# Time mixing with the inverse applied to the removal keys before the chain, and keys and removal keys stacked

## The chip, the cores and the metric

The kernel runs on one core of a Trainium2 chip. Its engines work side by side, each through its own queue in order: TensorE (PE, with its weight loads as PEld), VectorE (DVE), ScalarE (ACT), GpSimd (POOL), and SyncE (SP), which issues the transfers. The metric is the device time of one execution in microseconds (us). Lower is better.

## The reference

Two layers of a streaming encoder, over 64 frames of a running stream, 16 learned tokens and 1024 frames of a new stream. In each layer one projection feeds three groups of heads: a short gated convolution, latent attention, and RWKV-7 time mixing with four heads of 64. Their outputs go through one output projection. The change is in the time mixing, which is, per head and token:

```python
def step(s, inp):
    r_t, w_t, k_t, v_t, kk_t, a_t = inp
    sa = jnp.einsum('bhvk,bhk->bhv', s, -kk_t)
    s = (s * w_t[:, :, None, :] + sa[..., None] * (kk_t * a_t)[:, :, None, :]
         + v_t[..., None] * k_t[:, :, None, :])
    return s, jnp.einsum('bhvk,bhk->bhv', s, r_t)
```

The state `s` is decayed by `w`, loses what it holds along the removal key `kk`, gains `v` along `k`, and is read by `r`. A group norm over each head, a bonus term and a gate follow.

## The kernel before

Tokens are taken in chunks of 64. A pass (`rwkv_prep`, `rwkv_scan`, `rwkv_finish`) takes 384 tokens, which is six chunks, of two heads on 128 partitions. A layer has six passes: three token groups for each of two head pairs. Two layers make twelve passes and 72 chunks. Four of the chunks hold the learned tokens, which start from an empty state.

`rwkv_prep` forms, for the whole pass, the decays, the scaled removal keys `ar` (with the scaled `r` beside them), the keys `kt` and the write-back keys `bb`, and turns `v`, `bb` and `kt` so that tokens lie on partitions (`tm`, three transposes each). The products within a chunk are `x` (masked into `X1` for `bb` and `X2` for `kt`) and `av` (`X2` with the values). The triangular matrix in `X1` is inverted into `Q`: blocks of 16 on VectorE with a way through memory (`tri`), then block steps on TensorE (`inv`).

`rwkv_scan` then walks the six chunks in order. A chunk is a chain of three steps, each a visit to TensorE and one to VectorE. `xp` multiplies the removal keys with the state and adds `av`. `up` multiplies the inverse `Q` with that. `sp` multiplies the turned keys with `v` and the turned write-back keys with the result of `up`; VectorE adds the decayed state. At the end of the pass `yp` forms the output from the states (`ss`), `X2` with `v`, and `X1` with the results of `up`. These three share one PSUM bank (`rs`, one buffer); `rwkv_prep` uses two (`rw`).

The order is written by a planner while the program is built. `Meter` keeps a reckoned time for each engine. Time mixing is a set of side streams; each `yield` names the data and the bank that the next step needs. After each matmul of the main work, `pump` inserts the side steps whose needs are reckoned to be ready (`due`). The main work is the input projection of the layer (`prj`, 24 weight tiles of 128 columns and one smaller, in three token groups), and after it attention with the first half of the output projection (`race`). `self.solo` becomes true when the side streams are done, and gives attention more banks. `evict` copies out of PSUM on whichever of ScalarE and VectorE is reckoned to be free first.

Of the kernel before, what the change touches and what calls it, by code (L numbers as in the profile page):

```python
# [31 lines left out]
GN = 384  # L32
# [4 lines left out]
BLK = 16  # L37
# [154 lines left out]
class Net:  # L192
# [689 lines left out]
    def rwkv(self, l):  # L882

        parts = [(g, hp) for hp in range(2) for g in range(3)]
        self.state = [None, None]
# [24 lines left out]

    def rwkv_tag(self, i):
        return "z"

    def rwkv_prep(self, l, i, g, hp):
        nc, I, O = self.nc, self.I, self.O
# [15 lines left out]
        wa, wb = S("wa"), S("wb")  # L931
        e1, e2, a = (wa[:, GN * x:GN * (x + 1)] for x in range(3))
        ar = wb[:, 0:2 * GN].rearrange("p (i t) -> p i t", i=2)
        kk, rn, bb = wb[:, 0:GN], wb[:, GN:2 * GN], wb[:, 2 * GN:3 * GN]
        ch = lambda x: x.rearrange("p (c t) -> p c t", t=64)
        wt = S("wt")
        tm = [wt[:, GN * i:GN * (i + 1)] for i in range(3)]

        def turned(d, src):
# [20 lines left out]
        yield bb, "rw"  # L960
        turned(tm[0], v)
# [10 lines left out]
        for t in range(3):  # L972
# [5 lines left out]
        nc.gpsimd.tensor_copy(dc, ch(e1)[:, :, 63])  # L978
        yield a, kk, e2
        nc.vector.tensor_tensor(out=bb, in0=kk, in1=a, op=ALU.mult)  # L980
        nc.vector.tensor_tensor(out=bb, in0=bb, in1=e2, op=ALU.mult)
        nc.vector.scalar_tensor_tensor(out=ch(kk)[:, :, 1:64], in0=ch(kk)[:, :, 1:64], scalar=-1.0, in1=ch(e1)[:, :, 0:63],
                                       op0=ALU.mult, op1=ALU.mult)
        nc.vector.tensor_scalar(ch(kk)[:, :, 0:1], ch(kk)[:, :, 0:1], -1.0, None, op0=ALU.mult)
        nc.gpsimd.tensor_tensor(out=rn, in0=r, in1=e1, op=ALU.mult)
# [33 lines left out]
        chunks(X1, bb, C_X1)  # L1019
# [9 lines left out]
        chunks(X2, kt, C_X2)  # L1029
# [22 lines left out]
        spread = lambda x: x.unsqueeze(2).to_broadcast([128, 6, 4, BLK])  # L1052
# [6 lines left out]
        for y, d, o in ((1, dq, Q), (2, dt, Tm)):  # L1059
            nc.vector.tensor_tensor(out=o.rearrange("p t (b k) -> p t b k", k=BLK), in0=spread(d), in1=blk, op=ALU.mult)  # L1060
# [34 lines left out]
        yield (Q,)  # L1095
        self.made = dc, wb, wt, wq, wx

    def rwkv_scan(self, l, i, g, hp, dc, wb, wt, wq, wx):

        nc, I, O = self.nc, self.I, self.O  # L1100
        state = self.state
        rp = lambda s: self.ps(s, "rs")
        ar = wb[:, 0:2 * GN].rearrange("p (i t) -> p i t", i=2)
        vT, bT, kT = (wt[:, GN * i:GN * (i + 1)].rearrange("p (t f) -> p t f", t=3) for i in range(3))
        v4 = lambda x, n: x.rearrange("p (j t n) -> p j t n", j=2, n=n)
        X1, X2 = v4(wq[:, 0:768], 128), v4(wx[:, 0:768], 128)
        Q = X1[:, :, :, 0:64]
        AV, UU = v4(wq[:, 768:1152], 64), wx[:, 768:1152].rearrange("p (t f) -> p t f", t=3)
        quad = [(t, c) for t in range(3) for c in range(2)]
        cs = lambda t, c: slice(128 * t + 64 * c, 128 * t + 64 * c + 64)  # L1110
        cr = lambda c: slice(64 * c, 64 * c + 64)
        ss = self.S(self.rwkv_tag(i), "ss")[:, 0:768].rearrange("p (c n) -> p c n", n=128)
        nc.gpsimd.memset(ss, 0.0)
        for t, c in quad:
            ci = 2 * t + c
            sample, meta = g == 0 and ci == 0, g == 0 and ci == 1
            if sample:
                for j in range(2):
                    nc.sync.dma_start(ss[cr(j), 0, cr(j)], I["wkv"][l, hp, cr(j), :])
            elif ci == 0:  # L1120
# [390 lines left out]
```

## Time and profile before

| what | value |
|---|---|
| time, median of 3 runs | 1569.0 us (1568.38 to 1571.43) |
| the profiled execution | 1569.75 us |
| its span, first to last instruction | 1568.0 us |
| mean granted TensorE clock | 0.992 |
| HBM read and written | 81.24 and 36.60 MB |

The span is what the views of the profile divide; the rest of the profiled execution's time, 1.75 us, lies around it. Matmuls are pipelined: the length of one is not the time that it keeps the next from starting, so costs are best read from the distance between starts. A matmul of plain 32-bit floats is shown as two records, one of the rounded kind (`prj`) and a transpose as one.

### The profile page before, as it was taken

The numbers are of one execution on the slowest core, as the hardware profiler recorded it, in microseconds if no ns is written. First come the engines' busy times: TensorE is split into PE (matmuls) and PEld (weight loads), VectorE is DVE, ScalarE is ACT, GpSimd is POOL, SyncE is SP. The second block draws the span as 40 slices with busy tenths as digits, with TensorE's granted clock in tenths as the row PEclk, the third lists the DMA queues.
The fourth block names the chain that finished last, engine by engine and source line by source line (L and its number), as shares of the span: only waits on it lengthen the run. The fifth ranks groups of instructions, "written<-read, shape, count | busy, mean of one in ns | idle before, by whom it ended". The sixth has DMA issues, their size and how long they took to land. (4 is left out here: it accounts for less than half of the span.)

```text
span 1568.0 us, 31064 instructions
## 1 busy us (share of the span) xinstructions
PE 1507.0 (96%) x12304; PEld 1320.1 (84%) x12304; DVE 1029.5 (66%) x2569; ACT 745.1 (48%) x1752; POOL 276.5 (18%) x305
## 2 busy tenths in 40 slices
PE   7999999999999999999999999999999999999996
PEld 7988878988887777789999888798988877778896
DVE  7566575666758677575835575775676686576566
ACT  7125444334556565562522244434246575566442
POOL 0222222222221100100011222323122200011002
PEclk9999999999999999999999999999999999999998
DMA  6332122232225101122423311212312331002113
GB/s 215 121 100 70 53 56 58 62 57 73 82 78 173 36 26 39 59 66 61 149 88 102 108 44 53 72 44 77 56 56 80 105 127 46 27 29 77 53 64 116
DMA packets 95330, 119.84 MB, mean 76 GB/s; under 512 B 41873, under 2 KB 74769, under 8 KB 95185
## 3 DMA queue, kind: packets, MB, share of 16 engines
q1 hardware_dynamic: 95184, 117.87, 24.8%
q8 instruction: 96, 1.57, 0.4%
q14 instruction: 50, 0.40, 0.1%
HBM read 81.24 MB, written 36.60 MB: 75 GB/s over the span
## 5 line engine op out<-in xcount | busy, mean ns | idle before, releaser
L80 PE MATMUL prj<-hhi,whi 128*128 128x384 f32 (+1 forms) x1152 | 391.9, 340 | 7.5 <-ACT hhi L80 6.6
L80 PE MATMUL prj<-hhi,wlo 128*128 128x384 f32 (+1 forms) x1152 | 390.6, 339 | 0.5 <-DVE wlo L80 0.5
L80 PE MATMUL prj<-hlo,whi 128*128 128x384 f32 (+1 forms) x1152 | 388.3, 337 | 0.6 <-DVE hlo L80 0.6
L80 PEld LDWEIGHTS prj<-hhi,whi 128*128 128x128 f32 x1152 | 217.8, 189 | 12.6 <-ACT hhi L80 6.6
L80 PEld LDWEIGHTS prj<-hhi,wlo 128*128 128x128 f32 x1152 | 217.7, 189 | 5.6 <-DVE wlo L80 0.7
L80 PEld LDWEIGHTS prj<-hlo,whi 128*128 128x128 f32 x1152 | 218.0, 189 | 4.7 <-DVE hlo L80 1.0
L80 PE MATMUL prj<-yhi,wo 128*128 128x384 f32 (+2 forms) x776 | 207.9, 339 | 0.0
L80 PE MATMUL sc<-ka,qa 128*128 128x456 f32 (+9 forms) x720 | 152.4, 335 | 5.7 <-POOL qa L80 3.7
L80 ACT ACTIVATE p<-sc,st 128x144 f32<-128x144 f32 (+8 forms) x240 | 128.6, 544 | 50.4 <-DVE st L80 49.5
L80 PEld LDWEIGHTS prj<-yhi,wo 128*128 128x128 f32 x776 | 139.3, 189 | 3.1 <-DVE p L80 1.5
L80 DVE TENSOR_REDUCE st<-sc 128x1 f32<-128x456 f32 (+8 forms) x240 | 118.6, 503 | 34.4 <-PE sc L80 33.2
L80 PE MATMUL prj<-ylo,wo 128*128 128x384 f32 (+2 forms) x388 | 129.0, 332 | 0.0
L80 PEld LDWEIGHTS sc<-ka,qa 128*128 128x128 f32 (+1 forms) x720 | 111.0, 188 | 18.2 <-POOL qa L80 5.9
L80 ACT ACTIVATE pt<-tr 128x512 f32<-128x512 f32 (+3 forms) x174 | 92.7, 558 | 58.2 <-PE tr L80 57.3
L80 PE MATMUL tr<-cst,p 128*128 128x128 f32 (+2 forms) x752 | 113.8, 279 | 5.1 <-DVE p L80 2.6
L80 POOL TENSOR_TENSOR qa<-qt,qa 128x512 fp32r<-128x512 f32 (+1 forms) x40 | 47.7, 1195 | 363.4 <-ACT qa L80 362.9
L80 ACT ACTIVATE whi<-wraw 128x1024 fp32r<-128x1024 f32 x48 | 50.7, 1056 | 127.7 <-PE prj L80 117.4
L80 PEld LDWEIGHTS tr<-cst,p 128*128 128x128 f32 (+2 forms) x752 | 82.2, 141 | 27.1 <-ACT pt L80 10.1
L80 PE MATMUL po<-pt,v 128*64 128x256 f32 (+3 forms) x864 | 99.9, 355 | 0.1
L80 DVE TENSOR_TENSOR tri<-tri 48x14 f32<-48x14 f32 (+6 forms) x336 | 75.1, 223 | 17.5 <-DMA tri<-tri 7.7
L80 PEld LDWEIGHTS po<-pt,v 128*64 128x64 f32 (+1 forms) x864 | 56.6, 136 | 32.9 <-issue 8.7
L80 DVE TENSOR_SCALAR p<-p,st 80x336 f32<-80x336 f32 (+5 forms) x144 | 82.8, 575 | 1.5
(224 smaller groups left out, 2624.6 us busy)
## 6 DMA issues: line engine op xcount, KB each, us to landing
wraw<-w_in SPq DMA_DIRECT2D x48, 512.0 KB, 3.7
wraw<-w_out SPq DMA_DIRECT2D x32, 256.0 KB, 2.6
zd<-z SPq DMA_DIRECT2D x14, 576.0 KB, 3.5
wr<-zd SPq DMA_DIRECT2D x36, 192.0 KB, 2.6
gd<-gate SPq DMA_DIRECT2D x12, 552.0 KB, 2.9
yraw<-yd SPq DMA_DIRECT2D x8, 552.0 KB, 4.0
xn<-x SPq DMA_DIRECT2D x8, 552.0 KB, 4.0
xd<-xn SPq DMA_DIRECT2D x8, 552.0 KB, 2.8
```

What stands on the lines that cost most here:

```text
L80: r = f(*args, **kw)
```

## The change

The chain of a chunk goes from three steps to two. The inverse `Q` is applied for the whole pass in `rwkv_prep`: to the turned removal keys (`at`) and to `av`, in 24 products of 64x64x64 named `w`. `up` is gone, and its result comes straight out of `xp` and an addition. The 128 columns of `xp` now hold a chunk's removal keys beside its scaled `r`, so that the other half of its result is the state's part of the output; ScalarE copies that to `X2`. Keys `kt` and write-back keys `bb` of a chunk lie on opposite halves of the partitions (`kb`), likewise `v` and the chain's results (`uv`), so that `sp` is one product of 128x128x128 instead of four of 64x64x64. For this the chunks of `bb` and of the removal keys are written in swapped places, `X1` has its chunks swapped, and turned arrays are copied out of PSUM in two halves (`spread`). `yv` (`X2` with `v`, for the output) is formed beside `av`, `yp` keeps only `X1` with the chain's results, GpSimd adds the two other parts, and `rwkv_finish` starts with one more addition. The states are four fixed tiles that are cleared once.

```diff
+        def turned(src):
 
             ps = rp("tm")
             for t in range(3):
-                self.tr(ps[:, 128 * t:128 * (t + 1)], src[:, 128 * t:128 * (t + 1)], self.c(C_ID, 128))
-            nc.scalar.activation(d, ps[:, :GN], AF.Copy)
+                self.tr(ps[:, 128 * t:128 * (t + 1)], src(t), self.c(C_ID, 128))
+            return ps[:, :GN].rearrange("p (t f) -> p t f", f=128)
+
+        def spread(dst, ps, swap):
+
+            for x in range(2):
+                self.evict(dst[cr(x)].rearrange("p (t c f) -> p t c f", t=3, c=2)[:, :, 1 - x if swap else x, :], ps[cr(x)])
...
+        nc.vector.tensor_tensor(out=rn, in0=kk, in1=a, op=ALU.mult)
+        for c in range(2):
+            nc.vector.tensor_tensor(out=pair(bb)[:, :, 1 - c, :], in0=pair(rn)[:, :, c, :], in1=pair(e2)[:, :, c, :], op=ALU.mult)
+            nc.vector.scalar_tensor_tensor(out=ar[:, :, 1 - c, 1:64], in0=pair(kk)[:, :, c, 1:64], scalar=-1.0, in1=pair(e1)[:, :, c, 0:63],
+                                           op0=ALU.mult, op1=ALU.mult)
+            nc.vector.tensor_scalar(ar[:, :, 1 - c, 0:1], pair(kk)[:, :, c, 0:1], -1.0, None, op0=ALU.mult)
+        nc.gpsimd.tensor_tensor(out=ar[:, :, 2:6:3, :], in0=pair(r), in1=pair(e1), op=ALU.mult)
...
         yield bb, "rw"
-        turned(tm[1], bb)
+        spread(kb, turned(lambda t: bb[:, 128 * t:128 * (t + 1)]), True)
         yield kt, "rw"
-        turned(tm[2], kt)
-        vT, bT, kT = (d.rearrange("p (t f) -> p t f", t=3) for d in tm)
-        yield tm[2], rn, "rw"
-
-        wq, wx, wi = S("wq"), S("wx"), wa
+        spread(kb, turned(lambda t: kt[:, 128 * t:128 * (t + 1)]), False)
+        yield ar[:, :, 2:6:3, :], "rw"
+
...
+
+        uv = wr[:, 0:768]
+        uv6 = uv.rearrange("p (c f) -> p c f", f=128)
+        yield v, "rw"
+        spread(uv, turned(lambda t: v[:, 128 * t:128 * (t + 1)]), False)
+        yield ar, "rw"
+        nc.scalar.activation(at, turned(lambda t: wb[:, GN * t:GN * t + 128]), AF.Copy)
+        yield X2, uv, "rw"
         jtc = [(j, t, c) for j in range(2) for t in range(3) for c in range(2)]
-        ps = rp("av")
-        o = ps[:, :GN].rearrange("p (j t n) -> p j t n", j=2, n=64)
+        ps = [rp("av"), rp("yv")]
+        o = [x[:, :GN].rearrange("p (j t n) -> p j t n", j=2, n=64) for x in ps]
         for j, t, c in jtc:
-            self.mm(o[cr(c), j, t, :], X2[cr(c), j, t, 0:64], vT[cr(c), t, cr(j)], start=True, stop=True)
-        nc.scalar.activation(AV, o, AF.Copy)
+            for i in range(2):
+                self.mm(o[i][cr(c if i else 1 - c), j, t, :], X2[cr(c), j, t, 64 * i:64 * i + 64], uv6[cr(c), 2 * t + c, cr(j)],
+                        start=True, stop=True)
+        nc.scalar.activation(AV, o[0], AF.Copy)
+        nc.scalar.activation(X2[:, :, :, 64:128], o[1], AF.Copy)
...
-        yield (Q,)
-        self.made = dc, wb, wt, wq, wx
-
-    def rwkv_scan(self, l, i, g, hp, dc, wb, wt, wq, wx):
+        yield Q, AV, at, "rw"
+
+        ps = [rp("w"), rp("w")]
+        o = lambda c, j, x: ps[c][cr(j), 192 * x:192 * (x + 1)].rearrange("p (t n) -> p t n", n=64)
+        for j in range(2):
+            for t, c in quad:
+                b = cr(1 - c)
+                self.mm(o(c, j, 0)[:, t, :], at[b, t, cr(j)], X1[b, j, t, 0:64], start=True, stop=True)
+                self.mm(o(c, j, 1)[:, t, :], X1[b, j, t, 0:64], AV[b, j, t, :], start=True, stop=True)
+        for c in range(2):
+            self.evict(ar[:, :, 3 + c, :], ps[c][:, 0:192].rearrange("p (t n) -> p t n", n=64))
+            for j in range(2):
+                self.evict(AV[cr(1 - c), j], o(c, j, 1))
+        yield ar, AV
+        self.made = dc, wb, kb6, uv6, wq, wx
...
+            if meta:
+                nc.vector.tensor_copy(two(uv[b, ci, :]), QAV[b, :, t, :])
+            else:
+                yield s, "rs"
                 sd = self.small("sd", [128, 128])
-                nc.scalar.activation(sd, ss[:, ci, :], AF.Copy, scale=dc[:, ci:ci + 1])
-            xs = self.small("xs", [128, 128])
-            avc = AV[cr(c), :, t, :]
-            x3 = xs[cr(c), :].rearrange("p (j n) -> p j n", j=2)
-            if meta:
-                nc.vector.tensor_copy(x3, avc)
-            else:
+                nc.scalar.activation(sd, s, AF.Copy, scale=dc[:, ci:ci + 1])
                 ps = rp("xp")
-                self.mm(ps[:, 0:128], ar[:, 0, 128 * t:128 * (t + 1)], ss[:, ci, :], start=True, stop=True)
-                nc.vector.tensor_tensor(out=x3, in0=ps[cr(c), 0:128].rearrange("p (j n) -> p j n", j=2), in1=avc, op=ALU.add)
-            yield x3, "rs"
-            ps = rp("up")
-            for j in range(2):
-                self.mm(ps[cr(c), cr(j)], Q[cr(c), j, t, :], xs[cr(c), cr(j)], start=True, stop=True)
-            nc.vector.tensor_copy(UU[cr(c), t, :], ps[cr(c), 0:128])
-            yield UU[cr(c), t, :], "rs"
+                self.mm(ps[:, 0:128], wb[:, GN * t + 128 + 128 * c:GN * t + 256 + 128 * c], s, start=True, stop=True)
+                nc.vector.tensor_tensor(out=two(uv[b, ci, :]), in0=two(ps[b, 0:128]), in1=QAV[b, :, t, :], op=ALU.add)
+                nc.scalar.activation(X2[cr(c), :, t, 0:64], two(ps[cr(c), 0:128]), AF.Copy)
+            yield uv[b, ci, :], "rs"
             ps = rp("sp")
-            for x, y, z in ((kT, vT, True), (bT, UU, False)):
-                for j in range(2):
-                    self.mm(ps[cr(j), cr(j)], x[cr(c), t, cr(j)], y[cr(c), t, cr(j)], start=z, stop=not z)
+            self.mm(ps[:, 0:128], kb[:, ci, :], uv[:, ci, :], start=True, stop=True)
...
-            yield dst, "rs"
+            self.state = dst
+        nc.gpsimd.tensor_tensor(out=X2[:, :, :, 0:64], in0=X2[:, :, :, 0:64], in1=X2[:, :, :, 64:128], op=ALU.add)
+        yield uv, "rs"
 
         ps = rp("yp")
-        o = lambda t, c: ps[cr(c), 128 * t:128 * (t + 1)]
-        seen = set()
-        for t, c in quad:
-            if g or 2 * t + c != 1:
-                self.mm(o(t, c), ar[:, 1, cs(t, c)], ss[:, 2 * t + c, :], start=c not in seen, stop=False, group=False)
-                seen.add(c)
         for t in range(3):
             for j in range(2):
-                for i, (X, V) in enumerate(((X2, vT), (X1, UU))):
-                    for c in range(2):
-                        self.mm(o(t, c)[:, cr(j)], X[cr(c), j, t, 64:128], V[cr(c), t, cr(j)], start=False,
-                                stop=t == 2 and j == i == 1, group=False)
-        self.scanned = ps, wb, wx
-
-    def rwkv_finish(self, l, g, hp, ps, wb, wy):
-        nc, bon = self.nc, wb[:, 2 * GN:3 * GN]
-        y, sq, fm = wy[:, 0:GN], wy[:, GN:2 * GN], wy[:, 2 * GN:3 * GN]
+                for c in range(2):
+                    b = cr(1 - c)
+                    self.mm(ps[cr(c), 128 * t + 64 * j:128 * t + 64 * j + 64], X1[b, j, t, 64:128], uv[b, 2 * t + c, cr(j)],
+                            start=True, stop=True)
+        self.scanned = ps, wq, wx
...
+        tj = lambda x: x.rearrange("p (t j n) -> p t j n", j=2, n=64)
+        y0 = wx[:, 0:768].rearrange("p (j t n) -> p t j n", j=2, n=128)[:, :, :, 0:64]
+        nc.vector.tensor_tensor(out=tj(y), in0=tj(ps[:, :GN]), in1=y0, op=ALU.add)
+        nc.vector.tensor_reduce(out=gs[:, 0, :], in_=v6(y), op=ALU.add, axis=AX.X)
         nc.vector.tensor_scalar(gs[:, 0, :], gs[:, 0, :], 1.0 / 64, None, op0=ALU.mult)
-        nc.vector.tensor_tensor(out=v6(y), in0=v6(ps[:, :GN]), in1=b6(0), op=ALU.subtract)
+        nc.vector.tensor_tensor(out=v6(y), in0=v6(y), in1=b6(0), op=ALU.subtract)
...
+        self.states, self.turns_of_state = [self.cp.tile([128, 128], F32, name=f"state{i}") for i in range(4)], 0
+        for z in self.states:
+            nc.gpsimd.memset(z, 0.0)
```

TensorE in the first chunk of a pass, beside the projection `prj`; `ldp` and `icl` belong to the next pass. Before:

```order
L80 MATMUL xp_3352<-ss_3345,wb_2664 128x128
L80 MATMUL ldp_3368<-w_18_127,lora_3355 128x128 x3
L80 MATMUL icl_3376<-lora_3355,w_18_127 128x384
L80 MATMUL up_3382<-xs_3351,wq_2847 64x64 x2
L80 MATMUL prj_3340<-hlo_140,whi_3078 128x336
```

The same place with the change; `kkn` too belongs to the next pass:

```order
L80 MATMUL xp_2743<-state_128,wb_2052 128x128
L80 MATMUL ldp_2750<-w_18_135,lora_2731 128x128 x3
L80 MATMUL icl_2758<-lora_2731,w_18_135 128x384
L80 MATMUL prj_2720<-hlo_150,whi_2518 128x336
L80 MATMUL kkn_2768<-wq_2748,cst 128x384
L80 MATMUL sp_2764<-wr_1990,wt_2053 128x128
L80 MATMUL prj_2720<-hhi_142,wlo_2519 128x336
```

Between `xp` and `sp` no product by `wq`, the inverse, is left, `sp` reads `wr` and `wt` in one product, and it comes after one projection matmul, where before `sp` came twelve projection matmuls after `up`.

VectorE from the last step of the inverse (`inv`) to the state of the first chunk. Before:

```order
L80 COPY wa_1940<-inv_2579 32x6x32
L80 TENSOR_TENSOR wx_1511<-wx_1511,gs_2500 128x384
L80 COPY wq_2113<-inv_2617 32x6x32
L80 TENSOR_TENSOR xs_2649<-xp_2650,wq_2113 64x128
L80 TENSOR_TENSOR wb_2664<-ldp_2666,w0b_129 128x384
L80 COPY wx_2114<-up_2680 64x128
L80 SCALAR_TENSOR_TENSOR ss_2644<-sp_2695,dc_2011,sd_2647 64x64 x2
```

The same place with the change; `w` are the new products, `wr` holds values and the chain's results, `wq` the second factor that is added:

```order
L80 COPY wa_1400<-inv_1907 32x6x32
L80 COPY wq_1401<-inv_1927 32x6x32
L80 COPY wq_1401<-w_1947 64x192 x2
L80 COPY wq_1401<-w_1948 64x192 x2
L80 TENSOR_TENSOR wr_1390<-xp_1996,wq_1401 64x128
L80 TENSOR_TENSOR wx_2002<-ldp_2003,w0b_137 128x384
L80 SCALAR_TENSOR_TENSOR state_127<-sp_2017,dc_1460,sd_1994 64x64 x2
```

Four copies of `w` stand ahead of the chain, and the copy out of `up` is gone from it.

## Rows read from the trace of the kernel before

**Rows 1.** The page, busy time by engine: us, share of the span, instructions.
```profile
PE 1507.0 (96%) x12304; PEld 1320.1 (84%) x12304; DVE 1029.5 (66%) x2569; ACT 745.1 (48%) x1752; POOL 276.5 (18%) x305
```

**Rows 2.** The page, costliest groups: ScalarE halving a weight; busy, mean ns, idle before.
```profile
L80 ACT ACTIVATE whi<-wraw 128x1024 fp32r<-128x1024 f32 x48 | 50.7, 1056 | 127.7 <-PE prj L80 117.4
```

**Rows 3.** Busy us (and instructions) of PE, PEld, DVE, ACT, POOL by stretch; clock, DMA.
```profile
320.00:380.00 60.00, 57.99 (x582) 51.74 (x582) 38.26 (x97) 18.62 (x40) 14.04 (x17) 1.00 0.29 59
430.00:520.00 90.00, 86.36 (x635) 72.05 (x635) 63.72 (x168) 56.32 (x150) 16.92 (x17) 0.98 0.34 114
```

**Rows 4.** Waits of TensorE: us in total, times, longest us.
```profile
PE tm L80 <- DVE wb L80: 7.0, 8, 1.4
...
PE yp L80 <- DVE so L80: 5.7, 3, 2.7
...
PE up L80 <- DVE xs L80: 1.9, 5, 0.5
...
PE sp L80 <- DVE wx L80: 1.5, 2, 0.7
```

**Rows 5.** Timeline of TensorE around an `up`: start us, length us, group.
```profile
376.41 0.34 PE L80 MATMUL prj<-hhi,wlo 128*128 128x384 f32 x1
376.59 0.33 PE L80 MATMUL prj<-hhi,whi 128*128 128x384 f32 x1
376.85 0.44 PE L80 MATMUL up<-xs,wq 64*64 64x64 f32 x4
377.22 0.45 PE L80 MATMUL prj<-hlo,whi 128*128 128x384 f32 x1
377.51 0.34 PE L80 MATMUL prj<-hhi,wlo 128*128 128x384 f32 x1
```

**Rows 6.** Timeline of TensorE around an `sp`.
```profile
347.61 0.32 PE L80 MATMUL prj<-hhi,wlo 128*128 128x336 f32 x1
347.85 0.33 PE L80 MATMUL sp<-wt 64*64 64x64 f32 x4
...
348.49 0.32 PE L80 MATMUL prj<-hlo,whi 128*128 128x336 f32 x1
348.64 0.32 PE L80 MATMUL prj<-hhi,wlo 128*128 128x336 f32 x1
```

**Rows 7.** Timeline of TensorE around an `xp`.
```profile
352.05 0.33 PE L80 MATMUL prj<-hhi,wlo 128*128 128x384 f32 x1
352.22 0.38 PE L80 MATMUL xp<-ss,wb 128*128 128x128 f32 x2
...
352.62 0.34 PE L80 MATMUL prj<-hlo,whi 128*128 128x384 f32 x1
```

**Rows 8.** Timeline of TensorE, transposes `tm` with an `up` behind them.
```profile
264.36 0.49 PE L80 MATMUL tm<-cst,wa 128*128 128x128 f32 x3
...
265.43 0.34 PE L80 MATMUL prj<-hlo,whi 128*128 128x384 f32 x1
```

**Rows 9.** Timeline of TensorE in a `yp`.
```profile
300.27 0.88 PE L80 MATMUL yp<-ss,wb 128*64 128x128 f32 x12
301.07 0.33 PE L80 MATMUL yp<-wt,wx 64*64 64x64 f32 x4
301.24 0.28 PE L80 MATMUL yp<-wx,wq 64*64 64x64 f32 x4
...
302.40 0.28 PE L80 MATMUL yp<-wx,wq 64*64 64x64 f32 x4
```

**Rows 10.** Timeline of TensorE, an `x` and what follows it.
```profile
328.67 0.89 PE L80 MATMUL x<-wb 64*64 64x128 f32 x24
329.48 0.49 PE L80 MATMUL xp<-ss,wb 128*128 128x128 f32 x2
```

More of the change, by code (lines that the diff above doesn't have):

```diff
@@ L884, in rwkv @@
         parts = [(g, hp) for hp in range(2) for g in range(3)]
-        self.state = [None, None]
         made, begun, done = {}, set(), {}
@@ L909, in rwkv, with state_tile @@
         return [finish(), scan(), prep()]
+    def state_tile(self):
+        self.turns_of_state += 1
+        return self.states[self.turns_of_state % len(self.states)]
     def rwkv_tag(self, i):
@@ L930, in rwkv_prep @@
         hc = slice(128 * hp, 128 * hp + 128)
[L931 to L934, printed above, removed]
+        wa, wq, wx = S("wa"), S("wq"), S("wx")
+        third = lambda w, x: w[:, GN * x:GN * (x + 1)]
+        e1, e2, a = (third(wa, x) for x in range(3))
+        kk, rn, bb = third(wq, 0), third(wq, 1), third(wx, 2)
         ch = lambda x: x.rearrange("p (c t) -> p c t", t=64)
-        wt = S("wt")
-        tm = [wt[:, GN * i:GN * (i + 1)] for i in range(3)]
-        def turned(d, src):
+        pair = lambda x: x.rearrange("p (t c n) -> p t c n", c=2, n=64)
+        cs = lambda t, c: slice(128 * t + 64 * c, 128 * t + 64 * c + 64)
+        cr = lambda c: slice(64 * c, 64 * c + 64)
+        def turned(src):
             ps = rp("tm")
             for t in range(3):
-                self.tr(ps[:, 128 * t:128 * (t + 1)], src[:, 128 * t:128 * (t + 1)], self.c(C_ID, 128))
-            nc.scalar.activation(d, ps[:, :GN], AF.Copy)
+                self.tr(ps[:, 128 * t:128 * (t + 1)], src(t), self.c(C_ID, 128))
[3 more added lines that the diff above has]
+                self.evict(dst[cr(x)].rearrange("p (t c f) -> p t c f", t=3, c=2)[:, :, 1 - x if swap else x, :], ps[cr(x)])
         ps = rp("ldp")
@@ L978, in rwkv_prep @@
         nc.gpsimd.tensor_copy(dc, ch(e1)[:, :, 63])
+        wb, wt = S("wb"), S("wt")
+        ar = wb.rearrange("p (t s n) -> p t s n", t=3, n=64)
+        kb, at = wt[:, 0:768], third(wt, 2).rearrange("p (t f) -> p t f", t=3)
+        kb6 = kb.rearrange("p (c f) -> p c f", f=128)
         yield a, kk, e2
[L980 to L985, printed above, removed]
+        nc.vector.tensor_tensor(out=rn, in0=kk, in1=a, op=ALU.mult)
[5 more added lines that the diff above has]
+        nc.gpsimd.tensor_tensor(out=ar[:, :, 2:6:3, :], in0=pair(r), in1=pair(e1), op=ALU.mult)
         nc.vector.tensor_scalar(a, a, self.p(P_KA + hp), self.oka[:, hp:hp + 1], op0=ALU.mult, op1=ALU.add)
@@ L1002, in rwkv_prep, with chunks @@
         AV = v4(wq[:, 768:1152], 64)
-        A, Tm, Pm = (v4(wi[:, GN * i:GN * (i + 1)], 64) for i in range(3))
+        A, Tm, Pm = (v4(third(wi, i), 64) for i in range(3))
         quad = [(t, c) for t in range(3) for c in range(2)]
-        cs = lambda t, c: slice(128 * t + 64 * c, 128 * t + 64 * c + 64)
-        cr = lambda c: slice(64 * c, 64 * c + 64)
         msk = lambda x, n: self.c(x, n).unsqueeze(1).to_broadcast([128, 3, n])
-        def chunks(X, lhs, m):
+        arc = lambda t, c, j: ar[cr(j), t, 0:6:5, :] if c else ar[cr(j), t, 1:3, :]
+        def chunks(X, lhs, m, swap):
             pj = [rp("x0"), rp("x1")]
             for t, c in quad:
+                x = 1 - c if swap else c
                 for j in range(2):
-                    self.mm(pj[j][cr(c), 128 * t:128 * (t + 1)].rearrange("p (i n) -> p i n", i=2), lhs[cr(j), cs(t, c)],
-                                     ar[cr(j), :, cs(t, c)], start=True, stop=True)
+                    self.mm(pj[j][cr(x), 128 * t:128 * (t + 1)].rearrange("p (i n) -> p i n", i=2), lhs[cr(j), cs(t, x)],
+                            arc(t, c, j), start=True, stop=True)
             for j in range(2):
@@ L1018, in chunks @@
                     nc.scalar.activation(A[:, j], p3[:, :, 0:64], AF.Copy)
-        chunks(X1, bb, C_X1)
+        chunks(X1, bb, C_X1, True)
         dg = self.small("dg", [128, 6, BLK])
@@ L1028, in rwkv_prep @@
         yield X1, "rw"
-        chunks(X2, kt, C_X2)
+        chunks(X2, kt, C_X2, False)
         yield r, "rw"
@@ L1059, in rwkv_prep @@
         for y, d, o in ((1, dq, Q), (2, dt, Tm)):
-            nc.vector.tensor_tensor(out=o.rearrange("p t (b k) -> p t b k", k=BLK), in0=spread(d), in1=blk, op=ALU.mult)
+            nc.vector.tensor_tensor(out=o.rearrange("p t (b k) -> p t b k", k=BLK), in0=wide(d), in1=blk, op=ALU.mult)
         yield Q, Tm, "rw"
@@ L1116, in rwkv_scan @@
             sample, meta = g == 0 and ci == 0, g == 0 and ci == 1
+            b = cr(1 - c)
             if sample:
+                s = self.state_tile()
                 for j in range(2):
-                    nc.sync.dma_start(ss[cr(j), 0, cr(j)], I["wkv"][l, hp, cr(j), :])
-            elif ci == 0:
-                nc.vector.tensor_copy(ss[:, 0, :], state[hp])
-            if not meta:
-                sd = self.small("sd", [128, 128])
-                nc.scalar.activation(sd, ss[:, ci, :], AF.Copy, scale=dc[:, ci:ci + 1])
```

37 lines of the change are left out of this document (15 added, 22 removed).

## Prediction

> **What bounds the kernel now.** I read the page first: busy time by engine, then the costliest groups. TensorE is busy 96% of the span, VectorE 66%, ScalarE 48% [rows 1]. Matmuls overlap in their pipeline, so a busy TensorE is not yet a full one; the view by stretches and the waits have to say more. In the stretches in which time mixing runs, beside the input projection (320 to 380 us) and at the start of attention (430 to 520 us), TensorE is busy for 96 to 97%, and VectorE for 64 and 71% [rows 3]. The waits of TensorE are short: 7.0 us in all for the transposes `tm`, 5.7 for `yp`, 1.9 for `up`, 1.5 for `sp`, over both layers [rows 4]. The weights come early enough: ScalarE waits 117.4 us for TensorE to free a weight buffer [rows 2]. So TensorE's own queue is the bound, and time mixing, which is slipped between projection matmuls, costs what it takes of that queue. The chain from state to state costs nothing as latency while projections fill it; it costs the interruptions.
>
> What an interruption takes is read from starts, not from busy time. Projection matmuls of 384 columns start about 0.175 us apart, those of 336 columns 0.155 [rows 5, 6]. Over an `up` two starts of 384 columns lie 0.92 us apart, with two spacings of 0.175 in it: 0.57 us for `up` [rows 5]. Over an `sp`: 0.88 less 0.31, so 0.57 [rows 6]. Over an `xp`, one 128x128x128 product in two records: 0.57 less 0.35, so 0.22, or 0.11 a record [rows 7]. In the last part of `yp`, ten further groups of four records start in 1.16 us, 0.029 a record; these run in two halves of the array side by side, so one record of 64 columns alone takes 0.058 [rows 9]. Hence `up`, four records behind one another, has 0.23 us of work, `sp`, eight records two abreast, also 0.23; the other 0.34 us of each is what going from 128-wide tiles to 64-wide ones and back costs. It is no cheaper beside another 128-wide visit: three `tm` and an `up` take 1.07 less 0.175, and three records at 0.11 leave 0.57 [rows 8].
>
> **The change part by part.** Twelve passes (two layers, two head pairs, three token groups) of six chunks.
>
> *The product by the inverse leaves the chain.* 72 `up` go. In the order of the kernel before, 58 stand among 128-wide matmuls and 14 inside other 64-wide work: 58 x 0.57 + 14 x 0.23 = 36.3 us less.
>
> *Keys and removal keys stacked.* Four 64-wide products of `sp` become one of 128x128x128, the form of `xp`. 50 stood alone and gain 0.57 - 0.22 = 0.35, 17.5 us; the other 22 give 0.23 for 0.22, nothing.
>
> The Trainium skill, TensorEngine Tiling (Array Packing), section Theoretical Speedup, speaks against this step: contractions of at most 64 gain up to twice per small dimension from smaller tiles, so four quarter-array products should beat one full one that multiplies zeros. By that rule `sp` would have run four abreast, 0.12 us of work against 0.22, and the sum would be 7 us worse. The rows show two abreast and 0.23 us, so I leave the rule aside here.
>
> *The output.* `yp` loses the product with the state (ten or twelve records of 128 columns, 0.80 us to the next group) and half of its 48 small records: 0.80 + 1.45 us become 24 x 0.029 = 0.70, 18.6 us less over twelve [rows 9]. What is lost there comes out of `xp`, whose other 64 columns were thrown away before, at no TensorE time.
>
> *Added ahead of the chain.* `yv`, 24 records beside `av`: 12 x 24 x 0.029 = 8.4 us. The turned removal keys, three transposes: 12 x 0.33 = 4.0. The new products `w`, 24 of 64x64x64 in 48 records with their own change of tile size: 12 x (48 x 0.029 + 0.34) = 20.8. Their pattern isn't in the trace: two follow each other in one quarter of the array, then two in the other row half. Four abreast, as `x` does (24 records of 128 columns in 0.81 us, 0.034 each [rows 10]), would make it 8 us less; all behind one another (0.058) 17 us more. I take two abreast, since each quarter has two to do. By order, the remaining small groups are also interrupted more often, 110 runs of them for 84: 26 x 0.34 = 8.8 us.
>
> *Waits.* Three more steps of a pass can stall TensorE (turned removal keys, `av` with `yv`, `w`): 36 in all. At the mean of the 36 `tm` (7.0 us, so 0.2 each) that is 7 us; at none 0; at the longest `tm` wait seen, 1.4, it is 50. Against it stand 5.7 + 1.9 + 1.5 us at steps that go or shrink [rows 4]. I set both to cancel and keep -9 and +10 for the range.
>
> *At nothing.* VectorE loses 72 copies, gains half-width products, copies and a sum in front of the group norm; ScalarE gains a copy per chunk, GpSimd a sum per pass and loses its clearing of the states. VectorE's and ScalarE's idle third and half cover this [rows 1, 3]; without the cover it would show as TensorE waits, the second rival.
>
> Sum: 36.3 + 17.5 + 18.6 = 72.4 off, 8.4 + 4.0 + 20.8 + 8.8 = 42.0 on: 30.4 us less than the profiled execution's 1569.75 (span 1568.0; the median of the runs is 1569.0). That is 1539, and I say 1540.
>
> **The rivals.** *New small products run one behind another.* If both `w` and `yv` go at 0.058 per record, they cost 16.7 + 8.4 us more: 1565. For it: the unseen pattern of `w`. Against it: `yp` and `sp` keep two abreast with either half of the rows.
> The Trainium skill, same page, Gotcha 1 (PSUM Pressure), says that different row tiles cannot access one PSUM bank at the same time; `av` and `yv` each fill one bank from both row halves, so by it they would run singly. The trace disagrees: the 48 records of `yp` come from both row halves into one bank at 0.029 each.
>
> *`sp` waits for ScalarE; slower.* There is one `rs` bank. Before, only VectorE had to read `xp` before `sp` could take the bank; now ScalarE must copy the other half too, in a queue that holds weight halvings of 1.06 us [rows 2] and sigmoids. Behind a waiting `sp` every projection matmul stands. 68 such waits at one halving each are 72 us: 1612. It decides from 0.45 us a chunk on, where the gain is gone. Against it: the planner offers `sp` only when it reckons the bank free, and two of its reckonings on this chain erred by just 1.9 and 1.5 us over 72 chunks [rows 4].
>
> *The end of the last pass.* By order, three and a half chunks of a layer's last pass now come after the last projection instead of two, and attention gets its extra banks only after them. TensorE has 3.6 us not busy between 430 and 520 [rows 3]; should that treble, it is 7 us per layer, 1554.
>
> *The products stay, but the switches vanish unevenly*: if `w` runs four abreast and no new waits appear, 1540 - 8 - 9 = 1523.
>
> **How the numbers follow.** The forecast has a chance of 0.60 with its own range 1528 to 1554; products one behind another 0.08 (faster by a hair or the same); `sp` or other new waits eating the gain 0.14 (0.04 of it near the old time, 0.10 slower); the end of the pass 0.08; the deep case 0.10. A difference under 0.2%, 3 us, can't be told from none. That gives 0.82 faster, 0.08 same, 0.10 slower. The range leaves out half of the deep case and most of the slower one: 1520 to 1566.
>
> **What would show it.** `up` is absent; the starts around an `sp` lie 0.22 us further apart than without it, not 0.57; `yp` is 24 records in about 0.7 us; `w` takes 1.4 us of work; the waits of TensorE for `av`, `w` and `sp` stay under 10 us together. If `sp` waits for ScalarE show tens of us, or if the stretch beside the projections is not shorter by some 12 us per layer, the argument is wrong. So it is if TensorE turns out idle there: then the queue was no bound.

## The result, and the profile after

The changed kernel takes 1584.4 us (1581.7 to 1586.8, four runs) against 1568.7 for the one before: 1.0097 of its time, 95% interval 1.0076 to 1.0119. It is slower by 16 us, where 1540 us was forecast.

The page after, busy time by engine; it answers to [rows 1]:

```profile
PE 1493.1 (95%) x12060; PEld 1320.3 (84%) x12060; DVE 1063.8 (67%) x2605; ACT 781.1 (49%) x1884; POOL 282.3 (18%) x305
```

TensorE's work did fall, by 13.9 us. But the span grew by 11.8 us (1568.0 to 1579.8), so TensorE is not busy for 25.7 us more. VectorE has 34 us more to do, ScalarE 36. The waits of TensorE after say for whom it stands (us in total, times, longest); they answer to [rows 4]:

```profile
PE xp L80 <- DVE state L80: 12.2, 11, 2.2
PE ym L80 <- DVE wq L80: 10.2, 6, 3.0
PE yp L80 <- DVE state L80: 8.1, 6, 2.0
...
PE tm L80 <- DVE wx L80: 5.8, 6, 1.7
...
PE inv L80 <- DVE wa L80: 4.1, 4, 1.7
...
PE av L80 <- DVE wr L80: 3.0, 3, 1.8
PE sp L80 <- ACT wx L80: 2.8, 7, 0.7
```

The state that VectorE writes (`xp`, `yp`) and the finish (`ym`) are what comes late. The same steps before, beside those of [rows 4]:

```profile
PE ym L80 <- DVE wx L80: 1.3, 5, 0.3
...
PE inv L80 <- DVE wa L80: 0.7, 3, 0.4
...
PE xp L80 <- DVE ss L80: 0.4, 1, 0.4
```

ScalarE's copy ahead of `sp`, my slower rival, costs 2.8 us in all here: that rival is refuted for the changed kernel. It was the next to come, though: in a_gate, the fastest kernel below, it is the largest of these waits with 8.9 us.

The stretches after, columns as in [rows 3]:

```profile
140.00:200.00 60.00, 53.34 (x552) 47.88 (x551) 39.70 (x104) 31.04 (x72) 18.51 (x18) 1.00 0.20 57
...
320.00:380.00 60.00, 55.11 (x537) 50.73 (x536) 38.43 (x92) 20.45 (x46) 15.29 (x16) 0.97 0.26 51
...
430.00:520.00 90.00, 83.14 (x650) 68.43 (x650) 63.00 (x169) 57.12 (x155) 17.98 (x18) 0.94 0.35 114
```

The first of these stretches before:

```profile
140.00:200.00 60.00, 57.99 (x582) 50.04 (x581) 39.43 (x100) 26.71 (x59) 15.71 (x19) 1.00 0.19 51
```

TensorE, 96 to 97% busy in these three stretches before, is down to 89, 92 and 92%, and the granted clock slips to 0.97 and 0.94 in the last two. The input projections of the first layer, forecast to end some 12 us sooner, end 7.5 us later. Their last record before, and after:

```profile
458.33 0.34 PE L80 MATMUL prj<-hhi,wlo 128*128 128x384 f32 x1
```
```profile
465.84 0.34 PE L80 MATMUL prj<-hhi,wlo 128*128 128x384 f32 x1
```

In the second layer they end at 1227.3 and 1241.7 us, so another 7 us are lost there. The longest wait of `xp` shows how one wait is built. Here is the timeline around it, all engines (start us, length us, engine, group; in brackets the idle time before):

```profile
139.78 1.23 POOL L80 TENSOR_TENSOR wb<-wr,wa 128x384 f32<-128x384 f32 x1
...
140.07 2.23 DVE L80 SCALAR_TENSOR_TENSOR wb<-wq,wa 128x189 f32<-128x189 f32 x2
140.07 0.34 PE L80 MATMUL prj<-hhi,whi 128*128 128x384 f32 x1
...
140.25 0.38 PE L80 MATMUL sp<-wr,wt 128*128 128x128 f32 x2
...
140.65 0.34 PE L80 MATMUL prj<-hhi,wlo 128*128 128x384 f32 x1
...
140.97 1.11 POOL L80 TENSOR_TENSOR wr<-wr,wa 128x384 f32<-128x384 f32 x1
...
141.53 0.33 PE L80 MATMUL prj<-hlo,whi 128*128 128x384 f32 x1
...
142.22 0.61 DVE L80 TENSOR_TENSOR wx<-wq,wa 128x192 f32<-128x192 f32 x2
142.76 0.60 DVE L80 SCALAR_TENSOR_TENSOR wr<-wr,par 128x384 f32<-128x384 f32 x1
143.38 0.58 DVE L80 SCALAR_TENSOR_TENSOR state<-sp,dc,sd 64x64 f32<-64x64 f32 x2
...
144.10 0.46 PE L80 MATMUL xp<-state,wb 128*128 128x128 f32 x2 [2.25 <-DVE state L80]
```

`sp` ends about 140.6. VectorE could write the state then, but five instructions of the next pass's preparation stand ahead of it in its queue, the first of them begun. Two of them, the new half-width removal keys, take 2.23 us together while GpSimd runs two products. TensorE's last matmul ahead of `xp` starts at 141.53; `xp` starts at 144.10, and the projections behind it stand too.

The view by form shows that this is no single case (busy us, mean ns; then the idle time before):

```profile
L80 DVE SCALAR_TENSOR_TENSOR wb<-wq,wa 128x189 f32<-128x189 f32 x24 | 12.9, 547 | 0.0
...
L80 DVE TENSOR_TENSOR wx<-wq,wa 128x192 f32<-128x192 f32 x24 | 11.8, 506 | 0.1
```

Taken one by one, 16 of these 24 `wb` have no GpSimd product beside them and a median of 342 ns; the other 8 have one, and 1147 ns (two of them are not stretched). For `wx` it is 345 against 1165, for the 48-partition steps `tri` 196 against 885. The state update, which reads PSUM and one SBUF tensor, is 290 alone and 277 beside one: untouched. So most VectorE instructions with two SBUF inputs that run beside a GpSimd product stand until it ends. They are not the only ones: the `TENSOR_SCALAR` of attention's `p` (128x528, one tensor and a column) takes 484 ns alone and 1196 beside one. The sum of the stretch (each form's excess over its median alone, where it is above 150 ns) is about 56 us in some 80 places before and about 75 us in some 100 after. It is time of VectorE, not yet of the kernel.

The Trainium skill, SBUF — State Buffer, section "SBUF: two separate sides", states it: VectorE, with two SBUF inputs against a GpSimd instruction that reads SBUF or in a mode that takes both its port pairs, and GpSimd take one shared port pair as an exclusive lock; who starts first has it for the whole instruction, and the other blocks. The trace agrees, with the numbers above.

### The profile page after: what moved, and what is told of

It is laid out like the page before. It is cut to its first block, busy times and chain, and to the rows that moved or that the text cites. A ratio compares the mean times of both kernels' runs of the same rounds, so it can differ in the third digit from the quotient of the medians.

```text
span 1579.8 us, 30859 instructions
## 1 busy us (share of the span) xinstructions
PE 1493.1 (95%) x12060; PEld 1320.3 (84%) x12060; DVE 1063.8 (67%) x2605; ACT 781.1 (49%) x1884; POOL 282.3 (18%) x305
## 5 line engine op out<-in xcount | busy, mean ns | idle before, releaser
L80 PE MATMUL prj<-hlo,whi 128*128 128x384 f32 (+1 forms) x1152 | 393.1, 341 | 0.6 <-DVE hlo L80 0.6
L80 DVE TENSOR_TENSOR tri<-tri 48x14 f32<-48x14 f32 (+6 forms) x336 | 81.2, 242 | 19.3 <-DMA tri<-tri 9.4
L80 DVE TENSOR_TENSOR wlo<-wraw,whi 128x1024 fp32r<-128x1024 f32 x48 | 72.0, 1499 | 21.5 <-ACT whi L80 21.3
```

The costliest lines, as they stand in the source:

```text
L80: r = f(*args, **kw)
```

## The experiments

Every ratio is to the kernel before on the same chip; "us" is a median. "Waits" is the time TensorE stood over 0.15 us past the end of a record, summed; "bodies" is the rest of the distances between its starts. A slower clock is in the bodies. Both are of the one profiled execution, whose time can lie a few us off the median: that of the changed kernel took 1581.7 us.

An edit can also change the order that the planner writes. Counted in the traces, a_scalar and a_sum leave TensorE's order nearly as it is in the changed kernel (314 and 231 of 12060 records stand at another place), and b_dve that of the kernel before (156 of 12304). In a_vec it is 5128, in a_keys 2872, and from a_both to a_best, a_more and a_gate some 4000 to 8000 at each step. What these gain includes what another order gives or takes.

| kernel | us | ratio, 95% interval | waits | bodies |
|---|---|---|---|---|
| before | 1568.7 | | 43.2 | 1507.9 |
| changed | 1584.4 | 1.0097 (1.0076 to 1.0119) | 69.4 | 1494.1 |
| a_margin | 1605.6 | 1.0237 (1.0222 to 1.0252) | 76.8 | 1510.4 |
| b_margin | 1625.6 | 1.0373 (1.0350 to 1.0395) | 70.2 | 1542.7 |
| a_meter | 1591.0 | 1.0146 (1.0131 to 1.0161) | 79.5 | 1492.2 |
| b_meter | 1598.6 | 1.0205 (1.0183 to 1.0227) | 58.0 | 1520.4 |
| a_pace | 1586.5 | 1.0118 (1.0103 to 1.0133) | 71.2 | 1497.5 |
| b_pace | 1567.8 | 0.9997 (0.9987 to 1.0006) | 43.8 | 1504.1 |
| a_scalar | 1576.2 | 1.0055 (1.0040 to 1.0070) | 62.9 | 1493.7 |
| b_dve | 1585.6 | 1.0108 (1.0093 to 1.0124) | 53.7 | 1513.5 |
| a_vec | 1567.8 | 0.9989 (0.9977 to 1.0002) | 55.9 | 1491.1 |
| b_vec | 1567.5 | 0.9990 (0.9981 to 1.0000) | 40.8 | 1508.5 |
| a_sum | 1577.1 | 1.0050 (1.0035 to 1.0065) | 64.3 | 1495.7 |
| a_both | 1560.7 | 0.9948 (0.9934 to 0.9963) | 49.2 | 1493.3 |
| a_keys | 1581.4 | 1.0081 (1.0066 to 1.0096) | 67.5 | 1496.1 |
| b_keys | 1580.0 | 1.0075 (1.0060 to 1.0090) | 50.5 | 1511.2 |
| a_best | 1555.7 | 0.9923 (0.9907 to 0.9940) | 54.3 | 1482.1 |
| a_more | 1547.9 | 0.9857 (0.9829 to 0.9886) | 48.8 | 1479.3 |
| b_more | 1556.2 | 0.9927 (0.9910 to 0.9943) | 33.9 | 1503.5 |
| a_gate | 1544.0 | 0.9843 (0.9825 to 0.9861) | 49.4 | 1478.0 |

### Is it where the planner puts the steps?

```diff
-NEAR = 0.0
-LAZY = -1.3
+NEAR = -0.8
+LAZY = -2.0
...
-SIDE = -0.2
+SIDE = -1.0
```

a_margin: 

> The changed kernel with the same instructions, but the planner puts a step of time mixing into TensorE's order only when it reckons the inputs ready 1.0 us ahead (was 0.2; 2.0 instead of 1.3 where it is ahead of its pace, 0.8 instead of 0 for the steps that follow in one go). Theory A (TensorE stands because the steps stand in its order before VectorE has their inputs; the gaps over 0.6 us add up to 88 us, before 56): the gaps fall to 65 us or less and the time to 1545 to 1568. Theory B (the products and copies themselves cost more than the sum allowed): the gaps fall a little, the time stays at 1578 to 1590. Theory C (the chain as a whole is too long, every delay of a step ends at the end of the layer): slower than 1590.

b_margin: 

> The kernel before with the same three numbers, as the control. Theory A: its waits behind the side steps were small (about 17 us in four groups), so there is little to win and the chain with three steps per chunk is stretched: 1562 to 1580. Theory B: the same. If this kernel gains as much as the changed one (15 us or more), the margin is a matter of the planner alone and says nothing of the change.

```diff
-            cost, late = {"vector": 0.08 + n * 0.54e-3 if fast else 0.06 + n * 1.06e-3, ...
+            cost, late = {"vector": 0.2 + n * 0.58e-3 if fast else 0.2 + n * 0.95e-3, ...
```

a_meter (ScalarE's and GpSimd's figures are raised likewise): 

> The changed kernel with the same instructions, but the planner reckons with durations near to those of the trace: VectorE 0.20 us + 0.95 ns per element (was 0.06 + 1.06), ScalarE 0.18 + 0.86 (was 0.08 + 0.83), GpSimd's products 0.12 + 2.4 ns (was 1.7). Theory A: the steps are put in when their inputs are there, the gaps over 0.6 us fall to 65 us or less and the time to 1545 to 1568. Theory B: 1578 to 1590. Theory C: above 1590, the planner sees a longer chain and still cannot shorten it.

b_meter: 

> The kernel before with the same durations in its planner, as the control. Theory A: little to win, 1555 to 1575, and clearly less than what the changed kernel wins by the same edit. Theory B: no difference between the two kernels' gains.

All four are slower, by 7 to 57 us against their own kernel, and both controls lie above every range that was given for them. Caution does not cure the waits: in a_margin `yp` and `ym` wait 15.6 and 12.7 us for VectorE, more than in the changed kernel. Theory A as I had worded it here, a fault of placing alone, falls (in the runs below, Theory A is VectorE's queue), and Theory C's words come closest: what is put off comes back as waits further on. The controls lose more (57 and 30 us) than the changed kernel (21 and 7). Under either setting the changed kernel is the faster of the two, by 20.0 and 7.6 us.

```diff
-PACE = 3.4
+PACE = 3.2
```

a_pace: 

> The changed kernel with the planner's pace at 3.2 in place of 3.4 steps per piece of the projections, as its chain has 468 steps where that of the kernel before has 496. Theory A: no cure, 1578 to 1590. Theory D (each order is one draw, and small edits of the planner's numbers move the time by some 10 us either way): anywhere in 1565 to 1600, more than 4 us from 1584.

b_pace: 

> The kernel before with the same pace of 3.2. Theory A: 1565 to 1573. Theory D: slower by more than 4 us, as the numbers of the kernel before are those that gave it its short waits.

Both stay where they were (1586.5 against 1584.4, and 1567.8). In the first 5572 of TensorE's records stand at another place, in the second 1496. Theory D, that each order is a draw worth some 10 us, is not borne out by these two draws.

### Is it VectorE?

```diff
+    def evict_s(self, out, ps):
...
+        if nc.free["scalar"] < nc.free["vector"] + LEAN:
+            nc.scalar.activation(out, ps, AF.Copy)
+        else:
+            nc.nc.scalar.activation(out, ps, AF.Copy)
+            nc.note("vector", "tensor_copy", (out, ps), {})
```

The copies that the planner would have given to VectorE go to ScalarE, and the planner goes on counting them as VectorE's, so that the order stays.

a_scalar: 

> The changed kernel with the copies out of PSUM that the change brought (the turned keys, removal keys and values, and the two products of w) all on ScalarE, where half of them stood on VectorE; TensorE's order stays nearly that of the changed kernel. It takes some 26 us of work off VectorE (40 copies of 355 ns and 22 of 558) and puts it on ScalarE. Theory A (VectorE's queue in the preparation holds the chain's results back, and TensorE waits): the waits for VectorE's state, wq, wx and wa (40 us together) fall by half and the time to 1560 to 1575. Theory D (the waits come from where the planner happens to put the steps, whatever VectorE's load is): 1578 to 1592.

8.2 us of the loss go, with VectorE's busy time 26.6 us lower; the time is 1 us outside the range that I gave Theory A. Its waits fall from 40 us to 35 and not by half: `inv` no longer waits for `wa`, but `xp` still stands for 12.2 us, so it is not the copies that stand ahead of the state.

```diff
+            self.nc.nc.vector.tensor_reduce(out=self.spare, in_=x.rearrange("p (c n) -> p c n", n=64), op=ALU.add, axis=AX.X)
```

It runs five times in each preparation.

b_dve: 

> The kernel before with five more reductions of 128x384 on VectorE in every preparation (some 547 ns each, 60 in all, 33 us together; nothing reads them), of which the planner knows nothing, so that TensorE's order stays nearly that of the kernel before. It is the VectorE work by which the changed kernel exceeds the one before, without the change. Theory A: TensorE waits for VectorE's results, 8 to 25 us slower (1576 to 1593). Theory D: under 5 us slower (1566 to 1573).

The added group and two of TensorE's waits in b_dve:

```profile
L913 DVE TENSOR_REDUCE spare<-wt 128x6 f32<-128x384 f32 x36 | 19.7, 548 | 11.9 <-ACT wt L80 11.4 <-issue 0.2
...
L913 DVE TENSOR_REDUCE spare<-wq 128x6 f32<-128x384 f32 x24 | 13.1, 547 | 0.5
```
```profile
PE inv L80 <- DVE wa L80: 6.7, 5, 3.6
...
PE xp L80 <- DVE ss L80: 3.6, 5, 0.8
```

This is the clearest of the runs. The kernel before, with 32.8 us of VectorE work that nothing reads, becomes 17 us slower, as slow as the changed one, with TensorE's order nearly the same. More of the new waits come at `inv` (0.7 us before) than at `xp` (0.4). The added work itself is not stretched by GpSimd: a reduction takes 553 ns alone and 553 beside a GpSimd product. A microsecond of VectorE in the preparation costs half a microsecond of the kernel, though VectorE is idle for a third of the span. That price is an upper one: the first row shows that VectorE, its queue in order, also stood 11.4 us for the ScalarE copies that 36 of the reductions read; counted over work and standing, 44.2 us, it is 0.4.

### Is it GpSimd beside VectorE?

```diff
-nc.gpsimd.tensor_tensor(out=ar[:, :, 2:6:3, :], in0=pair(r), in1=pair(e1), op=ALU.mult)
+nc.vector.tensor_tensor(out=ar[:, :, 2:6:3, :], in0=pair(r), in1=pair(e1), op=ALU.mult)
```

and likewise k*a and the sum of the two parts of y.

a_vec: 

> The changed kernel with three 128x384 products of each preparation and chain moved from GpSimd to VectorE (r*e1, k*a and the change's own sum of the two parts of y). By the queue's plain load VectorE gets 36 instructions more of some 0.55 us, 20 us. Theory A (VectorE's load alone): half of it reaches the time, 1590 to 1597. Theory E (a product on GpSimd takes 1.0 to 1.2 us and stretches the instruction that VectorE runs beside it to its own end, some 0.8 us more, 75 us in 105 places of the changed kernel against 56 us in 83 of the one before): VectorE loses about as much stretch as it gets work, its busy sum rises by less than 8 us, and as the results no longer wait for GpSimd the time falls to 1570 to 1582.

b_vec (without the sum, which it doesn't have): 

> The kernel before with r*e1 and k*a on VectorE, as the control. Theory A: 13 us more of VectorE work, 1572 to 1578. Theory E: 1560 to 1570.

a_sum (the sum alone): 

> The changed kernel with only the change's own new GpSimd instruction, the sum of the two parts of y (12 of 1189 ns), moved to VectorE. Theory A: 6.6 us more of VectorE work, 1585 to 1589. Theory E: 1576 to 1584, and the stretch beside GpSimd falls from 75 us by about 8.

a_both (a_vec and a_scalar): 

> The changed kernel with the copies out of PSUM on ScalarE (1576.2 us by itself) and the three products on VectorE. Theory A: 1580 to 1588, the products cost what they cost alone. Theory E: both edits add up, 1560 to 1574; if the product's body saving is to show at all, it is here, at or under the kernel before (1568).

Moving work onto the engine that is late takes 16.6 us off (a_vec), 2 us more than Theory E had allowed. The rows of VectorE in a_vec, the three moved products and the two removal-key forms:

```profile
L80 DVE TENSOR_TENSOR wx<-wq,wa 128x192 f32<-128x192 f32 x24 | 9.5, 417 | 0.1
...
L80 DVE SCALAR_TENSOR_TENSOR wb<-wq,wa 128x189 f32<-128x189 f32 x24 | 8.4, 359 | 0.4
L80 DVE TENSOR_TENSOR wb<-wr,wa 128x384 f32<-128x384 f32 x12 | 8.3, 689 | 0.5 <-ACT wa L80 0.5
...
L80 DVE TENSOR_TENSOR wr<-wr,wa 128x384 f32<-128x384 f32 x12 | 6.6, 549 | 0.1
...
L80 DVE TENSOR_TENSOR wx<-wx 128x384 f32<-128x384 f32 x12 | 6.6, 548 | 0.1
```

The products take 21.5 us on VectorE, and its busy sum rises by 7.3 (1063.8 to 1071.1): the rest is mostly stretch that is gone, as the stretch counted as above falls from 75 to 62 us. On GpSimd one took 1.05 to 1.19 us, on VectorE 0.55 to 0.69. a_sum alone wins 7.2 us with the order nearly kept; the stretch falls there by some 4 us where I had said about 8. What these runs don't separate is the stretch from the simple delay: a sum that takes 0.55 us in place of 1.19 also lets the finish start sooner. The kernel before gains nothing that can be told from the two products (b_vec). With the copies on ScalarE too, a_both beats the kernel before by 8 us; there `xp` waits 6.6 us and `ym` 9.4:

```profile
PE ym L80 <- DVE wq L80: 9.4, 10, 1.3
...
PE xp L80 <- DVE state L80: 6.6, 15, 0.8
```

### Where did half of the saving in TensorE's work go?

Bodies fell by 13.8 us, not by 30. By kind, `up`, `sp` and `yp` lost 26.2, 10.6 and 19.8 us, and `w` and `yv` took 17.6 and 8.3. For `yp`, `w` and `yv` that is near what I had; of an `up` or `sp` a part lies in the bodies of the matmuls beside it. But the chunk products `x` grew from 20.1 to 29.6. The granted clock takes some more: its means, 0.992 over 1568.0 us and 0.988 over 1579.8, lie 12.5 and 19.0 us short of the full clock, 6 us more at most. The timeline of TensorE after shows why `x` grew, against the 24 records in 0.81 us of [rows 10]:

```profile
93.20 0.87 PE L80 MATMUL x<-wb,wx 64*64 64x128 f32 x12
94.00 0.43 PE L80 MATMUL prj<-hlo,whi 128*128 128x336 f32 x1
94.27 0.32 PE L80 MATMUL prj<-hhi,wlo 128*128 128x336 f32 x1
94.51 0.87 PE L80 MATMUL x<-wb,wx 64*64 64x128 f32 x12
95.31 0.42 PE L80 MATMUL prj<-hhi,whi 128*128 128x336 f32 x1
```

Twelve records take 0.80 us (93.20 to 94.00), as long as 24 did. Their starts come in twos and not in fours: only one head, so one row half of the array, is at work. Ten of the 24 groups of `x` are split so. The change had dropped the turned keys from what the step waits for, and the copies out of the `tm` bank still hold the second bank when `x` begins.

```diff
-        yield ar[:, :, 2:6:3, :], "rw"
+        yield kb, ar[:, :, 2:6:3, :], "rw"
```

a_keys: 

> The changed kernel, in which the first chunk products of a part wait for the stacked keys kb again, as they waited for the turned keys before the change; then both of their banks are free and the two rows of heads alternate in TensorE's order. Theory F (the dropped wait splits the products and costs a second group of 0.8 us in most of 12 visits): the bodies of `x` fall from 30 us to 24 or less and the time by 4 to 10 us, 1574 to 1580. Rival (the bodies of `x` are hidden behind waits for VectorE anyway): 1581 to 1590.

b_keys (the kernel before, heads written one after the other): 

> The kernel before with its first chunk products written by rows of heads, 12 and then 12, as the control. Theory F: these visits take 1.6 us in place of 0.82, 12 times, 7 to 11 us slower (1576 to 1580). Rival: under 3 us.

a_best (a_both with this wait): 

> The changed kernel with all three edits: copies on ScalarE, three products on VectorE, and the wait for the stacked keys. Theory F: 1549 to 1557, the edits add up (1560.7 without the wait). Rival: 1558 to 1563.

In a_best all `x` stand in groups of 24 again, and their bodies are 22.5 us for 32.2 in a_both:

```profile
L80 PE MATMUL x<-wb,wa 64*64 64x128 f32 x288 | 12.4, 279 | 2.7 <-ACT wa L80 2.7
L80 PE MATMUL x<-wb,wx 64*64 64x128 f32 x288 | 11.7, 278 | 0.0
```

That is worth 4.9 us there. In a_keys it is 3.0, which the intervals don't tell from nothing: 1581.4 lies in the range that I gave to the rival, although the bodies of `x` fell by 5.5 us. Those of the projections are 4.5 us longer there, at a clock of 0.985. So that the split costs bodies is shown; what it costs in time only a_best says, in another order. b_keys is inconclusive. It is 11 us slower, in the range of Theory F, yet its `x` grew by 1.8 us only, as the two heads stand right behind one another there (24 records in 1.08 us); 7.3 us of the rest are waits, in an order in which 5361 of 12304 records stand at another place.

### What is left

a_more (a_best with y + bonus on VectorE): 

> The same with one more product (y + bonus, 12 of 1085 ns on GpSimd) on VectorE. If what is left is still GpSimd's hold on VectorE: 2 to 5 us faster than a_best, and the stretch beside GpSimd under 60 us. If it is VectorE's load: 1 to 4 us slower than a_best.

b_more (the kernel before with r*e1, k*a and y + bonus on VectorE): 

> The kernel before with r*e1, k*a and y + bonus on VectorE, the three products of the mended kernel that the kernel before has too. If the lead of the mended kernel (1547.9) is the change's: 1563 to 1572, no or little gain, as with two of the three (1567.5). If it is GpSimd's products alone: 1548 to 1556.

a_gate (a_more with the product by the gate on VectorE): 

> The mended kernel with the product by the gate on VectorE as well (16 of 0.7 to 1.1 us on GpSimd), so that time mixing has no product left on GpSimd. Theory E: 1540 to 1547. If by now VectorE's own load weighs more: 1548 to 1554.

a_more wins 7.8 us more, over what I allowed, while the counted stretch does not fall (55 to 56 us). So this part is not shown to be the lock; that the finish no longer waits for GpSimd's queue would do as well. b_more lies on the upper edge of what I gave to GpSimd alone, 12.7 us under the kernel before. There y + bonus wins 11.3 us (b_vec to b_more), so none of that product's gain is the change's. Against b_more, a_more leads by 8.3 us, which includes its two other edits: its bodies are 24.2 us shorter and its waits 14.9 longer. a_gate is the fastest kernel by its median, 0.9843 of the one before, though its interval overlaps that of a_more. Its page:

```profile
PE 1476.1 (96%) x12060; PEld 1309.8 (85%) x12060; DVE 1042.3 (68%) x2602; ACT 807.0 (52%) x1951; POOL 220.5 (14%) x241
```

## Why the prediction was wrong

**The price of an interruption:** right. An `sp` after costs the 0.22 us forecast: over it two starts lie 0.58 apart (140.07 and 140.65), less two spacings of 0.175, so 0.23. `yp`, `yv` and `w` came out as worked out, 0.031 us a record for `w` (17.6 us for 576). In a_more the bodies are 28.6 us under those of before, against the 30.4 of the sum. That they come so near is in part luck, as b_more, without the change, has 4.4 of these us as well.

**TensorE's queue as the bound:** right for the kernel before, wrong for the changed one, by two signs that the prediction itself had named. In the three stretches shown above TensorE is not busy for 8 to 11% of the time, before for 3 to 4%, and the projections end later, not sooner. Another sign, waits for `av`, `w` and `sp` under 10 us together, held (5.8 us) and told nothing, as it looked at the wrong steps.

**The step that failed is "At nothing".** It priced VectorE's, ScalarE's and GpSimd's added work at zero, since idle thirds and halves would cover it. For ScalarE that held: 25 us more of it in a_scalar, and the time fell. For VectorE it did not. Its idle time is an average, and its queue is in order: what the preparation adds stands ahead of the chain's state update, and TensorE, in order too, stands behind `xp`. b_dve puts the price at 0.4 to 0.5, with the cover in place. The copies on VectorE that I counted as free cost 8.2 us (a_scalar), and the GpSimd sum 7.2 (a_sum). If the two add, which was not run by itself, they are the whole 16 us by which the changed kernel is slower than the one before.

**"Waits" failed with it.** I set new and old waits to cancel (-9 to +10); they grew by 26.2 us. I looked for them at the steps that the change adds (`tm`, `av`, `w`), and those took 8.8 us (5.8 and 3.0, none for `w`), where `tm` alone had 7.0 before. The rest came at `xp`, `ym` and `yp`, which existed before: 30.5 us in place of 7.4. How much of it goes when VectorE and GpSimd are relieved the runs show (48.8 us of waits in a_more), but not why a_more keeps 14.9 us more than b_more.

**Two terms were missing.** The dropped wait for the turned keys splits `x`: 9.5 us of bodies that the sum does not hold. And the mean granted clock was lower, 6 us at most; by the stretches at the end of this text it can fall after a wait.

**The rivals.** Products one behind another: no, `w` and `yv` went two abreast. `sp` behind ScalarE: 2.8 us for 72. The end of the last pass: no. From the end of the input projections to the first projection of the second layer it is 322.2 us before and 322.1 after, and to the end of the kernel 340.7 and 338.1; all that is lost is lost beside the projections.

By runs, the 44 us between forecast and result go like this: copies and products on other engines 23.7 (a_both), the wait for the keys 4.9 (a_best), GpSimd's two last products 11.7 (a_more, a_gate), which leaves 4.0. These are differences of medians, most with another order of TensorE. The kernel before can have the part of y + bonus as well (b_more), so that part is no measure of the change: with the same products on VectorE, the change is worth 8.3 us, and not 30.

## What to carry to other kernels

An engine that is idle a third of the time covers nothing by that: ask what stands behind the added instruction in its queue and who waits for that. A product moved to GpSimd to relieve VectorE is little relief if VectorE then reads two SBUF tensors beside it; compare an instruction's mean duration with that of its twins of the same shape, which showed this already before the change. When a diff drops an operand from a wait, look for what that wait also kept in order.

## What the runs showed of the hardware

The sign was in the trace before. Two VectorE groups of one shape and operation, both with two SBUF inputs. `wb`, issued next to GpSimd's two products, takes 889 ns and `acc` 554; of the 24 `wb`, 14 are stretched, by 8.0 us together. I had read neither row:

```profile
L80 DVE TENSOR_TENSOR acc<-acc,sqt 128x384 f32<-128x384 f32 x41 | 22.7, 554 | 5.8 <-ACT sqt L80 5.1
...
L80 DVE TENSOR_TENSOR wb<-wb,wa 128x384 f32<-128x384 f32 x24 | 21.3, 889 | 1.7
```

And a wait can cost more than itself. Stretches of 2 us after the 3.05 us for which `ym` stood until 432.62 in the changed kernel (columns as in [rows 3]):

```profile
430.00:432.00 2.00, 0.00 (x0) 0.00 (x0) 1.94 (x5) 0.60 (x3) 0.99 (x1) 1.00 0.54 131
432.00:434.00 2.00, 1.38 (x13) 1.08 (x15) 0.89 (x2) 0.47 (x1) 0.00 (x0) 0.62 0.99 331
434.00:436.00 2.00, 2.00 (x18) 1.88 (x15) 0.68 (x3) 1.76 (x5) 1.00 (x1) 0.50 0.14 50
436.00:438.00 2.00, 2.00 (x8) 2.00 (x7) 0.18 (x1) 1.56 (x4) 1.26 (x2) 0.50 0.00 0
438.00:440.00 2.00, 2.00 (x20) 1.75 (x21) 0.00 (x0) 0.00 (x0) 0.61 (x1) 0.68 0.26 97
440.00:442.00 2.00, 2.00 (x47) 1.93 (x44) 0.75 (x2) 1.31 (x3) 0.00 (x0) 1.00 0.01 2
```

TensorE stood, and then the granted clock was 0.50, the lower level of 1.2 GHz, until about 439 us. Over these four stretches that is 2 x (0.38 + 0.50 + 0.50 + 0.32) = 3.4 us at most, about as much as the wait itself. Not every hole is followed by that: the one of 2.25 us ahead of 144.10 lies in a stretch with a clock of 1.00. The mean clock tells the same: 0.992 before, 0.988 in the changed kernel, 0.975 in b_margin.
